# Attention with bias: score matmuls of two query chunks, whole transposes for pair 2 and the rests of q, shared output tiles, a new order

## The chip, the core and the metric

The kernel runs on one core of a Trainium2 chip. Its engines are named as on the profile's page: PE multiplies matrices (PEld are its weight loads, which run beside it), DVE and ACT compute elementwise, POOL computes elementwise too and here mostly issues transfers, and SP issues transfers. The metric is the device time of one execution in microseconds (us). Of a profiled execution there is also the span, from the first to the last instruction on the core.

## What is computed

Attention with an additive bias, for 4 batches of 8 heads, 1024 queries and keys, head dimension 64, in float32:

```python
scores = scale * np.matmul(q, k.transpose(0, 1, 3, 2))      # scale = 1 / 8
scores = scores + bias                                      # one bias for all heads
attn = np.exp(scores - scores_max) / (sum + 1e-8)
return np.matmul(attn, v)
```

## The kernel before

**Tiles.** Heads are taken in 16 pairs; each head's 1024 queries are 8 chunks of 128, and one unit of work, a *slot*, is one chunk of one head against all 1024 keys: 256 slots. PE multiplies keys by queries into PSUM as scores with the keys on the partitions, 8 blocks of 128 keys by 128 queries, which fill two PSUM banks (four blocks each). ACT takes the exponential of both banks into the ring `E` of 28 half slots (14 slots). PE then multiplies each block by the values: 8 matmuls of 65 columns, 64 of V and a column of ones that gives the row sums. Seven slots' outputs or fewer share one PSUM bank (`SIZES`); DVE takes the reciprocal of the sums, scales the bank and SP stores it.

**Bias.** A slot's bias is not added for each head. The operands of a head carry differences to the head before, so that scores build up in the banks: a first head of a group gets its bias by 8 matmuls with `ident8` (line 360), and every later head adds the product of two heads' stacked operands to what stands in the bank (line 363, `start=False`). So each pair needs four arrays of 128 rows by 1024: `ko`, `qo` (its own k and minus its q for the odd head) and `ke`, `qe` (stacked with the neighbour pair's), and for some pairs `qs` and `qz`. A place (0, 1 or 2) is a pair of banks, and three slots, a *round*, are under way at once. Slots 0 to 53 are the first pass (three chunks of the first 18 heads), slots from 54 on come after it.

**Preparing operands.** POOL loads k, q and v as bf16. Up to pair 6, k and q land with the two heads apart, and must be set side by side before a whole 128-column transpose: either DVE copies them into a `side` tile (`set_beside`, line 303), or PE transposes each head by itself (line 276, 64 columns, two instructions a block). From pair 7 on they land side by side. PE's transposes (line 270) go to PSUM, DVE copies them out as `ko` (line 284) or `qo` (line 286), and `ke`, `qe` are made by DVE copies (lines 295 and 297) or by SP's transfers (line 579). The chunks 3 to 7 of q of pairs 0 and 1 are loaded later, as rests.

**DVE's exponentials.** 29 of the 256 slots get their exponential from DVE in six steps: lines 401, 409, 413, 416, 419 and 422, the last of which writes the tile `de`.

**Order.** All engines work through their instructions in the order in which they are issued, and this order is a list of tokens written out in `ORDER`. `F` and `G` fill a slot's first and second bank; `X` is ACT's exponential of a slot, `P` and `Q` those of one and a half slots; `f r s h c l` are DVE's six steps; `A` is a slot's output matmuls; `T`, `C`, `D`, `S`, `N` are a transpose, its copy out, a doubling into `ke` or `qe`, a side copy and a negation, with `k` or `q` (or `r`, a rest) and the pair; `V` copies a landed v into place; `R` and `M` are a bank's reciprocal and scaling. Ahead of the list stands a head written out by hand (lines 482 to 532). POOL limits the loads under way: before a load it copies one element of an earlier one into `tick` (line 547).

## Time and profile before

| what | us |
|---|---|
| median of 3 runs (lowest, highest) | 226.67 (225.88, 227.08) |
| the profiled execution's own time | 226.95 |
| its span | 225.2 |
| ACT's first exponential begins, last one ends | 8.26, 220.06 |
| PE, DVE, ACT, POOL busy in the span | 215.4, 203.4, 212.5, 89.5 |

A row of the page gives the line, the engine, the operation, what it writes and reads with the shapes, the count, then busy time and the mean of one in ns, then idle time in front of it and what ended that. A row of a timeline gives start, length and the same names. A stretch's row gives its bounds, its length, each engine's busy time with the count of instructions that touch it, the granted clock of PE as a share, and figures of the transfers.

### The profile page before, as it was taken

Reading aid. Unit: us, or ns where it says so; the run is one execution under the profiler, and the core shown is the slowest. Engines: PE = TensorE matmul, PEld = TensorE weight load, DVE = VectorE, ACT = ScalarE, POOL = GpSimd, SP = SyncE. Lnnn points to the kernel's source line nnn. Section 1 sums busy time; section 2 is a strip of 40 time slices with the busy share of each in tenths; the row PEclk is TensorE's granted clock in tenths of the full one; section 3 lists DMA queues with packets and bytes.
Section 4 is the critical chain, followed back from the end, with each engine's and each line's share of the span. In section 5 each row is a group of like instructions: output and inputs, shape, how many; then the busy total and the mean of one; then the engine's idle time right before and its main releaser. Section 6 shows DMA issues by size and latency. Waiting matters only on the chain.

```text
span 225.2 us, 10307 instructions
## 1 busy us (share of the span) xinstructions
PE 215.4 (96%) x4535; PEld 206.5 (92%) x4535; DVE 203.4 (90%) x349; ACT 212.5 (94%) x225; POOL 89.5 (40%) x160
## 2 busy tenths in 40 slices
PE   7999999999999999999999997999999999999991
PEld 2879989999999999999999897999999999999891
DVE  3488798796999999999999999999999999999992
ACT  3799999999999999999999997999999999999990
POOL 8817568757557556306476653650000000000000
PEclk9999999999999999999999999999999999999998
DMA  6999999999999999899999999997112110212213
GB/s 197 217 205 215 230 216 156 188 172 174 140 123 150 108 132 97 114 151 175 167 183 202 116 185 177 97 154 77 45 45 58 27 42 20 73 39 66 56 50 100
DMA packets 88141, 28.95 MB, mean 129 GB/s; under 512 B 69216, under 2 KB 84832, under 8 KB 88096
## 3 DMA queue, kind: packets, MB, share of 16 engines
q0 software_dynamic: 62880, 14.06, 69.2%
q1 hardware_dynamic: 24512, 13.38, 23.4%
q10 hardware_dynamic: 704, 0.85, 1.2%
q8 instruction: 35, 0.57, 1.1%
q14 instruction: 10, 0.08, 0.1%
HBM read 29.36 MB, written 8.39 MB: 168 GB/s over the span
## 4 chain that ended last, share of the span: by engine, by line
ACT 32%; PE 9%; DVE 5%; DMA 5%; POOL 1%; issue 1%; DVEq 0%; POOLq 0%
ACT E L382 32%; PE pl L363 5%; PE po L443 4%; DMA k<-in_k_dram 3%; DMA q<-in_q_dram 2%; DVE dy L401 1%; DVE ds L413 1%; POOL tick L547 1%; DVE ob L475 1%; DVE qo L286 1%; POOL q L202 1%; DVE de L416 1%; DVE de L409 0%; DVE ko L284 0%; DVE q L309 0%
## 5 line engine op out<-in xcount | busy, mean ns | idle before, releaser
L382 ACT ACTIVATE E<-pl 128x1024 bf16<-128x1024 f32 (+2 forms) x221 | 209.4, 1075 | 3.4 <-PE pl L363 2.1
L443 PE MATMUL po<-vall,E 128*128 128x65 bf16 x1816 | 85.8, 194 | 0.1
L363 PE MATMUL pl<-qo,ko 128*128 128x128 bf16 x1024 | 77.5, 219 | 0.7 <-ACT E L382 0.6
L443 PEld LDWEIGHTS <-E 128*128 128x128 bf16 x1816 | 73.3, 98 | 0.3 <-DVE vall L628 0.2
L363 PEld LDWEIGHTS <-ko 128*128 128x128 bf16 x1160 | 68.5, 98 | 2.9 <-ACT E L382 1.1
L363 PE MATMUL pl<-qe,ke 128*128 128x128 bf16 x888 | 68.0, 219 | 1.4 <-issue 1.2
L363 PEld LDWEIGHTS <-ke 128*128 128x128 bf16 x888 | 51.9, 98 | 3.0 <-issue 1.6
L401 DVE TENSOR_SCALAR dy<-pl 128x1024 int32<-128x1024 f32 x29 | 35.3, 1218 | 2.8 <-PE pl L363 1.9
L422 DVE SCALAR_TENSOR_TENSOR de<-dy,ds 128x1024 uint16<-128x1024 int32 x29 | 34.9, 1213 | 0.0
L475 DVE TENSOR_TENSOR ob<-po,rs 128x448 f32<-128x448 f32 (+2 forms) x38 | 22.8, 601 | 0.5
L409 DVE TENSOR_SCALAR de<-dy 128x1024 f16<-128x1024 uint16 x29 | 19.6, 689 | 0.6 <-PE po L443 0.5
L202 POOL DMA_DIRECT2D q<-in_q_dram x18 | 15.9, 883 | 10.5 <-DVE qo L286 8.2
L413 DVE TENSOR_TENSOR ds<-de 128x1024 f16<-128x1024 f16 x29 | 19.6, 678 | 0.1
L419 DVE TENSOR_TENSOR ds<-ds,de 128x1024 f16<-128x1024 f16 x29 | 19.5, 679 | 0.1
L202 POOL DMA_DIRECT2D k<-in_k_dram x18 | 15.8, 880 | 8.1 <-PE px L270 4.7
L243 POOL DMA_DIRECT2D vall<-in_v_dram x18 | 16.8, 934 | 4.3 <-issue 3.6
L284 DVE COPY ko<-px 128x1024 bf16<-128x1024 bf16 (+1 forms) x16 | 10.7, 668 | 4.7 <-PE px L270 2.8
L286 DVE TENSOR_SCALAR qo<-px,sgn 128x1024 bf16<-128x1024 bf16 (+2 forms) x18 | 12.3, 684 | 2.5 <-PE px L270 1.5
L360 PE MATMUL pl<-ident,braw 128*128 128x128 bf16 x136 | 13.9, 227 | 0.0
L416 DVE TENSOR_SCALAR de<-de 128x1024 f16<-128x1024 f16 x29 | 13.0, 454 | 0.1
L443 PE MATMUL po<-vall,de 128*128 128x65 bf16 x232 | 12.1, 194 | 0.4 <-DVE ob L475 0.4
L360 PEld LDWEIGHTS <-braw 128*128 128x128 bf16 x136 | 11.1, 148 | 0.1
(63 smaller groups left out, 144.7 us busy)
## 6 DMA issues: line engine op xcount, KB each, us to landing
ke<-ko SPq DMA_DIRECT2D x20, 128.0 KB, 4.2
out_dram<-ob SPq DMA_DIRECT2D x40, 64.0 KB, 3.4
k<-in_k_dram POOLq DMA_DIRECT2D x18, 128.0 KB, 5.3
q<-in_q_dram POOLq DMA_DIRECT2D x18, 128.0 KB, 4.5
vall<-in_v_dram POOLq DMA_DIRECT2D x18, 128.0 KB, 5.4
out_dram<-ob SPq DMA_DIRECT2D x62, 32.0 KB, 2.6
braw<-in_bias_dram POOLq DMA_DIRECT2D x7, 256.0 KB, 5.4
v<-in_v_dram POOLq DMA_DIRECT2D x7, 256.0 KB, 6.3
```

The lines of the kernel that those rows point to most:

```text
L202: nc.gpsimd.dma_start(out=t[:, :, y, :], in_=(qf, kf)[x][pr][:, y].rearrange("p (c d) -> p c d", d=D))
L243: nc.gpsimd.dma_start(out=vall[:, (2 * pr + t) % VR, :, :D], in_=vf[pr][:, t])
L360: m = nc.tensor.matmul(to, braw[:, c, :].rearrange("p (kp kc) -> p kc kp", kc=NCH)[:, kc, :], ident8[:], start=i == 0, stop=False, skip_gr ...
L363: m = nc.tensor.matmul(to, kk[:, kc, :], qq[:, c, :], start=False, stop=True, skip_group_check=True)
L382: read(nc.scalar.activation(E[:, e0:e0 + n].rearrange("p b x -> p (b x)"), pl[:, b0:b0 + n].rearrange("p b x -> p (b x)"), ACTF.Exp, scale ...
L401: read(w.tensor_scalar(t["y"][:], pl[:, b:b + 2].rearrange("p b x -> p (b x)"), scale * LOG2E * 65536.0, CB * 65536.0, op0=ALU.mult, op1=A ...
L409: w.tensor_scalar(t["f"], t["lo"], CA / 65536.0, CA * CR, op0=ALU.mult, op1=ALU.add)
L413: w.tensor_tensor(t["s"], t["f"], t["f"], op=ALU.mult)
L419: w.tensor_tensor(t["s"], t["s"], t["f"], op=ALU.mult)
L422: w.scalar_tensor_tensor(t["e"].bitcast(U16).rearrange("p c q -> p (c q)"), t["y"][:], 1.0 / 512.0, t["s"], op0=ALU.mult, op1=ALU.add)
L443: nc.tensor.matmul(bank[b][:, banks[b].index(s), :], ehalf[s, kc // 4][:, kc % 4, :], vall[:, slots[s][2] % VR, kc, :], start=first and kc ...
L475: nc.vector.tensor_tensor(ob[:, :n, :], po[:, :n, :D], rs[:, :n, :].to_broadcast([P, n, D]), op=ALU.mult)
```

## The change

From slot 54 on, the slots of places 0 and 1 of a round are a *couple*: two neighbouring query chunks of one head. Place 0's banks now hold key blocks 0 to 3 of both chunks and place 1's banks blocks 4 to 7 of both. One score matmul has 256 moving columns, the two chunks, against one weight load. There are 68 such couples. An exponential covers half of the keys of both chunks, and an output's eight matmuls read both slots' exponentials.

```diff
+    couple = {}
     for s, x in enumerate(slots):
+        if s >= 6 * GROUPS[0] and x[0] < 2:
+            couple[s] = rounds[round_of[s]][:2]
...
+        n = 2 if s in couple else 1
+        if n == 2:
+            c = slots[couple[s][0]][1]
+        k0 = 4 * x + 2 * b if n == 2 else 4 * b
         for i in range(4):
-            kc = 4 * b + i
+            kc, c1 = k0 + i // n, c + i % n
...
+            elif i % n == 0:
+                m = nc.tensor.matmul(pl[:, 2 * x + b, i * P:(i + n) * P], kk[:, kc, :],
+                                     qq[:, c:c + n, :].rearrange("p c q -> p (c q)"), start=i == 0 and order[0] == "s",
+                                     stop=order[1] == "s", skip_group_check=True)
...
+    def weights(s, kc):
+
+        if s not in couple:
+            return ehalf[s, kc // 4][:, kc % 4, :]
+        return ehalf[couple[s][kc // 4], kc % 4 // 2][:, kc % 2 * 2 + couple[s].index(s), :]
```

Pair 2's k and q and the rests of q get side copies (`S`, now with a piece's chunks) and whole transposes; only pair 1 keeps the 64-column form. V's landings and DVE's output tiles share one pool of seven, in place of three and four. The tick copies go; a load's own issue waits for the earlier one. Loads of the second bias chunk and of pair 1's k change places.

```diff
-    def set_beside(pr, which):
+    def set_beside(pr, which, c0, n):
...
-    de = ctx.enter_context(tc.tile_pool(name="de", bufs=4))
+    de = ctx.enter_context(tc.tile_pool(name="de", bufs=7))
...
-            lands[pr, "v"] = vland.tile([P, 2, NCH, D], BF, name="v16")
+            lands[pr, "v"] = de.tile([P, NCH, P], BF, name="de").rearrange("p c q -> p (c q)").rearrange(
...
+                flight.append(do().ins)
                 if j >= 0:
-                    nc.gpsimd.tensor_copy(tick[:], flight[j])
-                flight.append(do())
+                    tc.add_manual_dep(flight[i], flight[j].name, DATA, reason="loads under way")
```

In the head, the cast of the second half of pair 0's k is split between ACT and DVE, the exponential's dependence on the ko copy is declared away, and the second round's exponential is taken bank by bank, its scores ahead of its bias. `ORDER` and `SIZES` are new throughout; the list's start as an example:

```diff
-F1 G1 F2 X1 G2 F3 X2 G3 Tk1a F4 X3 Ck1 G4 Tq1b F5 Dk1p0 X4 G5 Cq1 Tk2a Dq1p0 Dq1p1 X5 F6 Ck2 G6 F7 G7 X6 Tq2b F8 Cq2
+F3 G3 Tk1a X3 F4 Ck1 G4 F2 X4 Dk1p0 Tq1b G2 Cq1 Dq1p0 X2 Dk1p1 F6 G6 Sk2 X6 F5 G5 F7 Tk2a X5 G7 Sq2 F9 X7 Ck2 F8 G8
...
+        if not on:
+            tc.declare_no_dep(i, group="p", reason="another bank")
...
-        nc.scalar.copy(kr0[1].rearrange("p c t d -> p t c d"), k0f[:, :, half:])
+        nc.scalar.copy(kr0[1][:, :2].rearrange("p c t d -> p t c d"), k0f[:, :, half:half + 2])
...
+        nc.vector.tensor_copy(kr0[1][:, 2:].rearrange("p c t d -> p t c d"), k0f[:, :, half + 2:])
...
+        fill_half(1, 0, "s", "sb")
         fill_half(0, 1, "s")
         exp((0, 1))
+        fill_half(1, 0, "b", "sb")
+        exp((1, 0))
+        fill_half(1, 1, "s", "sb")
+        fill_half(1, 1, "b", "sb")
+        exp((1, 1))
```

In the rows below, what stands in brackets are the engines and queues for which an instruction waits. In the head, ACT's list before, from its first cast on (`dy` holds the landed inputs, `braw` the bias, `de` the cast k, `pl` the scores):

```order
L511 CAST braw<-dy 128x1024 [waits DMAHW1_49]
L512 CAST de<-dy 128x2x4x64 [waits DMAHW3_49]
L382 ACTIVATE E<-pl 128x512 [waits DVE_49,PE_49]
L382 ACTIVATE E<-pl 128x512 [waits PE_49]
L382 ACTIVATE E<-pl 128x1024 [waits PE_49] x20
```

and in the change:

```order
L513 CAST braw<-dy 128x1024 [waits DMAHW1_49]
L514 CAST de<-dy 128x2x2x64 [waits DMAHW3_49]
L382 ACTIVATE E<-pl 128x512 [waits PE_49] x4
L382 ACTIVATE E<-pl 128x1024 [waits PE_49] x14
L382 ACTIVATE E<-pl 128x1024
```

The cast of k is half as long, the first exponential no longer waits for DVE, and four short exponentials stand where there were two. The other half of that cast stands on DVE, ahead of the first `ko` copy:

```order
L512 CAST de<-dy 128x2x4x64 [waits DMAHW2_49]
L519 TENSOR_SCALAR qz_94<-px 64x384 [waits PE_49]
L520 CAST de<-dy 128x2x2x64 [waits DMAHW3_49]
L274 COPY ko<-px 128x512 [waits PE_49]
L274 COPY ko<-pl 128x512 [waits PE_49]
```

L520 is new there; the other four stood in this order before. On PE, at the start of the second pass, the end of a group of score matmuls (`ko` are the weights, `qo` the moving queries, `pl` the scores), before:

```order
L363 MATMUL pl<-qo,ko 128x128
L363 LDWEIGHTS ko
L363 MATMUL pl<-qo,ko 128x128
L443 LDWEIGHTS E
L443 MATMUL po<-vall,E 128x65 [waits DVE_49]
```

and in the change:

```order
L359 MATMUL pl<-qo,ko 128x256
L359 LDWEIGHTS ko
L359 MATMUL pl<-qo,ko 128x256
L359 LDWEIGHTS ko [waits Activation_49]
L359 MATMUL pl<-qo,ko 128x128
```

A couple's bank takes two matmuls of 256 columns; a slot of place 2 behind it still takes 128. On DVE, near the end of the first pass, where the rests of q come in (`vall` holds V in place, `dy` and `de` belong to DVE's exponentials, `po` is an output bank), before:

```order
L628 COPY vall<-v_259 128x16x64 [waits DMASW4_49]
L401 TENSOR_SCALAR dy<-pl 128x1024 [waits PE_49]
L286 TENSOR_SCALAR qo<-px,sgn 128x640 [waits PE_49]
L468 RECIPROCAL rs<-po 128x7
L297 TENSOR_SCALAR qz_98<-qo 64x640 [waits DVE_49]
L297 TENSOR_SCALAR qe<-qo 64x640
```

and in the change:

```order
L635 COPY vall<-de 128x16x64 [waits DMASW4_49]
L470 RECIPROCAL rs<-po 128x7 [waits PE_49]
L401 TENSOR_SCALAR dy<-pl 128x1024 [waits PE_49,Activation_49]
L477 TENSOR_TENSOR ob<-po,rs 128x448 [waits DMAHW6_49,DVE_49]
L293 COPY side<-qrest_251 128x2x5x64 [waits DMASW5_49]
L409 TENSOR_SCALAR de<-dy 128x1024
L413 TENSOR_TENSOR ds<-de 128x1024 [waits DVE_49]
L276 TENSOR_SCALAR qo<-px,sgn 128x640 [waits PE_49]
L287 TENSOR_SCALAR qz_94<-qo 64x640 [waits DVE_49]
L287 TENSOR_SCALAR qe<-qo 64x640
```

The side copy of the rest is new, and two steps of a DVE exponential now stand between it and `qo`. In the whole list PE has 7932 rows in place of 9072, and the 70 tick copies of POOL are gone.

More of the change, by code (lines that the diff above doesn't have):

```diff
@@ L133 @@
     warm = consts.tile([P, 1], F32)
-    tick = consts.tile([1, 1], BF)
     sgn = consts.tile([P, 1], F32)
@@ L176 @@
     assert sorted(x[1:3] for x in slots) == sorted((c, h) for c in range(NCH) for h in range(2 * NP))
-    first_slot = {}
-    last_slot, last_of = {}, {}
+    rounds = {}
+    for s, r in enumerate(round_of):
+        rounds.setdefault(r, []).append(s)
+    couple = {}
     for s, x in enumerate(slots):
-        first_slot.setdefault(x[2] // 2, s)
-        last_slot[x[2] // 2] = s
-        last_of[x[2]] = s
-    before = {}
-    at_place = {}
-    for s, x in enumerate(slots):
-        before[s] = at_place.get(x[0])
-        at_place[x[0]] = s
+        if s >= 6 * GROUPS[0] and x[0] < 2:
+            couple[s] = rounds[round_of[s]][:2]
+    assert all(slots[a][1:] == (slots[b][1] - 1,) + slots[b][2:] for a, b in couple.values())
     raws, lands, arrs = {}, {}, {}
@@ L223, in piece @@
             to = t[:, :, :cs.stop - cs.start, :]
-            nc.gpsimd.dma_start(out=to.rearrange("p t c d -> p t (c d)"),
-                                in_=qf[pr][:, :, cs.start * D:cs.stop * D])
-            return to[:1, 1, cs.stop - cs.start - 1, D - 1:]
+            return nc.gpsimd.dma_start(out=to.rearrange("p t c d -> p t (c d)"),
+                                       in_=qf[pr][:, :, cs.start * D:cs.stop * D])
         return [piece]
```

157 lines of the change are left out of this document (73 added, 84 removed).

## The prediction

> **What bounds the kernel now.** I read the page's busy shares first, then the groups by shape.
>
> ```profile
> span 225.2 us, 10307 instructions
> PE 215.4 (96%) x4535; PEld 206.5 (92%) x4535; DVE 203.4 (90%) x349; ACT 212.5 (94%) x225; POOL 89.5 (40%) x160
> L382 ACT ACTIVATE E<-pl 128x1024 bf16<-128x1024 f32 x205 | 189.8, 1053 | 2.4 <-PE pl L363 2.1
> L382 ACT ACTIVATE E<-pl 128x1536 bf16<-128x1536 f32 x14 | 19.2, 1473 | 0.0
> ```
>
> Three engines stand at 90% or more, so no share alone decides. ACT does little but exponentials, and its idle time in front of them is 2.4 us. How fast could it run? The next view cuts its time at every twelfth exponential (the count also takes in the two at the edges, so x14 holds twelve); the last row, from a second cut, holds five of the wide ones.
>
> ```profile
> 8.26:9.35 1.09, 1.09 (x3) 1.00 1.17 195
> 9.35:20.60 11.25, 11.13 (x14) 1.00 1.25 209
> 20.60:31.53 10.93, 10.93 (x14) 1.00 1.22 223
> 31.53:43.13 11.60, 11.11 (x14) 1.00 1.73 179
> 43.13:54.91 11.78, 11.47 (x14) 1.00 1.39 181
> 122.16:133.61 11.45, 11.21 (x14) 1.00 1.42 158
> 133.61:145.89 12.28, 11.11 (x14) 1.00 1.32 140
> 156.94:167.87 10.93, 10.93 (x14) 1.00 0.19 47
> ...
> 203.77:210.44 6.67, 6.67 (x6) 1.00 0.27 75
> ```
>
> The best stretches give 10.93 / 12 = 0.911 us for an exponential of 1024 columns and 6.67 / 5 = 1.334 for 1536. At that pace the 205 and 14 would need 186.8 + 18.7 = 205.5 us, and the two short ones took 1.09. From 8.26 to the last exponential's end at 220.06 there are 211.8, so **about 5.2 us are lost on ACT**, 8.3 lie before it and 5.1 behind. Against 10.93 the rows lose 0.32, 0.67 and 0.85 in the first pass (with 0.24 more up to 66.08: 2.1 in all), then 0.52 and 1.35 around 122 to 146; the other 1.2 is spread thinly. The chain of waits shows the largest:
>
> ```profile
> 128.69 0.26 PE po L443 x8
> 128.95 0.45 PE px L270 x8
> ...
> 138.41 0.17 PE pl L363
> 138.58 1.20 issue
> 139.78 0.58 PE pl L363 x7
> 140.38 63.37 ACT E L382 x68
> ```
>
> PE stopped for 1.20 us inside a group of eight score matmuls and waited for nothing that the profile shows; from 140.38 ACT alone carries the chain for 63 us. So the change can win only the 5.2 us, plus what it does to the head and the tail.
>
> **The head.**
>
> ```profile
> 6.62 0.62 ACT L512 CAST de<-dy 128x512 bf16<-128x512 f32 x1 [0.47 <-DMA dy<-in_k_dram]
> 6.80 0.42 DVE L284 COPY ko<-px 128x512 bf16<-128x512 bf16 x1 [0.23 <-PE px L270]
> 7.30 0.40 PE L270 MATMUL pl<-ident,de 128*128 128x128 bf16 x4
> 7.53 0.39 PE L363 MATMUL pl<-qz,ko 128*128 128x128 bf16 x4
> 7.73 0.42 DVE L284 COPY ko<-pl 128x512 bf16<-128x512 bf16 x1 [0.51 <-PE pl L270]
> 8.26 12.44 ACT L382 ACTIVATE E<-pl 128x512 bf16<-128x512 f32 x14 [1.01 <-DVE ko L284]
> ```
>
> The first exponential waits for the second ko copy although its own matmuls end at 7.92. The changed ACT list names PE alone there, which is worth 8.26 - 7.92 = 0.34. The cast at 6.62 is halved between ACT and DVE: ACT ends some 0.3 earlier, DVE puts about 0.28 (0.42 for 512 columns, halved, plus something fixed) ahead of its copy at 6.80, and 0.23 of that was idle. The transposes so start near 7.0, not 7.30; but the matmuls then wait for that copy, near 7.3, which leaves about 0.2 of the 0.3. The first two rounds become four short exponentials, 1.09 / 2 = 0.55 each against 0.91 for a whole one: 0.2 lost. I take **-0.45 us for the head** (bounds -0.6 and 0) and +0.2 for ACT's own work, in which 207 exponentials, 12 wide ones and four short ones need 188.6 + 16.0 + 2.2 = 206.8 against 186.8 + 18.7 + 1.1 = 206.6.
>
> **PE's work.**
>
> ```profile
> 1.20 4.37 PE L500 MATMUL pl<-E 128*128 128x512 bf16 x10 [1.20 <-DVE warm L488]
> 12.59 0.64 PE L276 MATMUL px<-ident,k 128*64 128x128 bf16 x16
> 17.84 0.61 PE L270 MATMUL px<-ident,side 128*128 128x128 bf16 x8
> ```
>
> From slot 54 on, 68 couples of slots with eight keys' blocks each turn 1088 score matmuls of 128 columns into 544 of 256. No row shows 256. The chain has 0.45 / 8 = 56 ns for 128 columns and 0.26 / 8 = 32 for 65. Two of 128 bound the new one at 112; a line through the two points gives 104; the 512-column form took 437 in the first 5 us, half of it 218. That last is far off: it would add 58 us, and columns went at 0.85 ns there against 0.44 later, so the place sets it rather than the width. I take 110, nearest to the 128-column row: 544 x 2 ns = 1.1 us (0 to 4.4). PE also drops 1140 rows of its list, 9072 to 7932. The whole transposes take 0.61 for what took 0.64: 52 half ones become 26, some 0.1. PE so saves **about 1.2 us out of 209**, thin over 150 us.
>
> Here a page says otherwise. The Trainium skill, "TensorE: Matmul & The Clock Gate", section "Back-to-back issue gap", gives 81 ns a matmul at 128 columns and 131 at 512 where each has its own weight load; an estimate from it for 256 is 98, so a couple would save 64 ns and PE 35 us. The trace disagrees: its loaded 128-column matmuls go at 56. By that page nothing would remain of ACT's waits on PE, which is the second case below.
>
> **DVE's work and the first pass.**
>
> ```profile
> 20.60:66.08 45.48, 44.39 (x933) 42.76 (x930) 39.06 (x76) 44.62 (x50) 28.70 (x57) 1.00 1.36 177
> 66.08:220.06 153.98, 152.09 (x3339) 149.80 (x3335) 151.62 (x241) 152.54 (x160) 47.40 (x79) 1.00 0.84 104
> ```
>
> ```profile
> L401 DVE TENSOR_SCALAR dy<-pl 128x1024 int32<-128x1024 f32 x29 | 35.3, 1218 | 2.8 <-PE pl L363 1.9 <-issue 0.2
> L422 DVE SCALAR_TENSOR_TENSOR de<-dy,ds 128x1024 uint16<-128x1024 int32 x29 | 34.9, 1213 | 0.0
> L409 DVE TENSOR_SCALAR de<-dy 128x1024 f16<-128x1024 uint16 x29 | 19.6, 689 | 0.6 <-PE po L443 0.5
> L413 DVE TENSOR_TENSOR ds<-de 128x1024 f16<-128x1024 f16 x29 | 19.6, 678 | 0.1
> L419 DVE TENSOR_TENSOR ds<-ds,de 128x1024 f16<-128x1024 f16 x29 | 19.5, 679 | 0.1
> L475 DVE TENSOR_TENSOR ob<-po,rs 128x448 f32<-128x448 f32 x30 | 18.6, 619 | 0.4
> L416 DVE TENSOR_SCALAR de<-de 128x1024 f16<-128x1024 f16 x29 | 13.0, 454 | 0.1
> L303 DVE COPY side<-q 128x1024 bf16<-128x1024 bf16 x4 | 2.2, 538 | 0.0
> ```
>
> DVE's third column in the first row says 39.06 busy of 45.48 us. Between the same exponentials (the 13th to the 60th) the new list has two side copies more and a V copy less (together 0.54), one closing pair (0.62 and a short one), and of DVE's own exponential one step each of L401, L409 and L413, two each of L416, L419 and L422: 0.54 + 0.62 + 1.22 + 0.69 + 0.68 + 0.91 + 1.36 + 2.43 = 8.4. Two L419 in a row take 1.28 where twice 0.68 would be 1.36, so about 0.08 of each overlaps; less 0.9, **+7.5**.
>
> ```profile
> 61.27 1.28 DVE L419 TENSOR_TENSOR ds<-ds,de 128x1024 f16<-128x1024 f16 x2
> ```
>
> That makes 46.6 in a stretch of 45.5: DVE is full. I cost this at nothing, because the outputs of slots 30 and 47 come 27 and 12 exponentials after their last steps in the new list, so chain steps may run late; what may not are the doublings (D), which stand one exponential, 0.9 us, ahead of the score matmuls that read them. If the cover is gone it costs up to 1.1 plus the waits that DVE cannot avoid, of 6.4 idle now. In return DVE has those 7.5 us less behind 66.08, where it is 151.62 of 153.98 busy. There ACT loses 3.1: the 1.2 us stop of PE, for which I take -0.9 (0 to -1.2: it is the only one of its length, and nothing shows why it should return or not), and 1.9 of thin losses, of which I take half, -1.0 (0 to -1.9), for a PE lighter by 1.2 and a DVE lighter by 7.5.
>
> The 70 tick copies on POOL go, and loads wait at their own issue; POOL is 40% busy, so nothing (if the loads come early, -0.3). V's landings in seven shared tiles take nothing: a load no longer waits for a V copy three loads back. Four stores and one ke copy more sit on SP's queue, hidden behind stores that nobody reads. The tail is the same: one output, reciprocal, scaling, store.
>
> **Sum against the profiled run:** 226.95 - 0.45 + 0.2 + 0 - 0.9 - 1.0 = 224.8. The profiled run lies 0.28 above the median of 226.67, so **224.5 on the median**, -1.0%. A measurement of this kernel can tell about 0.5%, 1.1 us, from no change.
>
> **Rivals.**
> - **ACT alone is the bound.** All 5.2 us go: 226.67 - 0.45 + 0.2 - 5.2 = 221.2. For it: DVE and PE get room behind 66 us. Against: the first pass gets none.
> - **The gain is hidden.** PE's 1.2 us are no one's last wait; the stop returns, and what the later part wins the full DVE takes in the first pass: head and ACT alone give -0.25, 226.4 (225.6 to 227.8).
> - **DVE becomes the bound from 20 to 66 us.** 46.6 of work plus half of its 6.4 idle is 49.8, so this stretch grows by 4.3: 226.67 - 2.15 + 4.3 = 228.8. It decides when D copies come over 0.9 us late; slower than before begins where DVE's waits there exceed 45.5 + 2.15 - 46.6 = 1.0 us beyond what late chain steps absorb. Against: at 151.62 of 153.98 it has run full behind 66 us with 3.1 lost in 154.
>
> **Chances:** forecast (223 to 226) 0.45; ACT alone 0.17; hidden 0.22; DVE bound 0.16. Below 225.5 fall most of the first and all of the second, 0.55; within 0.5% 0.28; above 227.8 0.17. The range 221.3 to 228.6 leaves about one in ten on each side, and takes in the bounds of the terms.
>
> **What would show it.** Right: the first exponential near 7.8; 256-column matmuls 108 to 112 ns apart; from 66 to 220 twelve exponentials in 10.95 or less; no stop of over 1 us on PE. Wrong: score matmuls in the first pass whose releaser is a DVE doubling or side copy; twelve exponentials in over 11.6 between 30 and 66; ACT waiting for outputs because both exponentials of a couple must be done; a couple's matmuls above 112 ns.

## The result, and the profile after

The changed kernel takes **227.63 us** (median of 9 runs, 226.78 to 228.91) against 226.67 of the kernel before in 9 runs beside it: ratio 1.0051, 95% interval 1.0028 to 1.0074, slower by half a per cent. The profiled execution took 227.62 with a span of 225.5, against 226.95 and 225.2. The direction was predicted wrong. The time lies in the stated range and in that of the rival "the gain is hidden" (225.6 to 227.8), about as far from its 226.4 as from the 228.8 of the rival "DVE becomes the bound".

The page's busy shares after, with the group of ACT's whole exponentials:

```profile
span 225.5 us, 9039 instructions
PE 215.3 (95%) x3965; PEld 197.5 (88%) x3965; DVE 206.3 (91%) x354; ACT 213.0 (94%) x227; POOL 72.5 (32%) x90
L382 ACT ACTIVATE E<-pl 128x1024 bf16<-128x1024 f32 x207 | 192.6, 1067 | 2.7 <-PE pl L359 2.2 <-PE po L445 0.3
```

The program has 1268 instructions fewer. ACT's idle time in front of whole exponentials, 2.4 us before, is 2.7. The two stretches whose DVE time the prediction worked out (bounds, length, then busy time of PE, PEld, DVE, ACT and POOL):

```profile
20.60:66.08 45.48, 44.46 (x905) 42.95 (x903) 44.69 (x88) 44.35 (x48) 25.05 (x30) 1.00 1.38 182
66.08:220.06 153.98, 152.09 (x2789) 140.05 (x2787) 147.74 (x231) 152.68 (x161) 34.64 (x39) 1.00 0.83 103
```

DVE went from 39.06 to 44.69 in the first and from 151.62 to 147.74 in the second: the shift of work happened. Between the same exponentials as in the prediction (the 13th to the 60th, here at 21.07 and 67.10) DVE is busy 45.24 of 46.03 us, so it has 6.2 more to do and not 7.5. PE's 152.09 behind 66 us did not move, though its list is shorter. ACT alone, cut at every 24 halves of `E` (twelve whole exponentials; the count also takes in those at the edges):

```profile
21.97:33.05 11.08, 11.08 (x13) 1.00 1.26 227
33.05:45.43 12.38, 11.56 (x13) 1.00 1.69 171
45.43:56.83 11.40, 11.13 (x13) 1.00 1.28 166
...
134.31:145.73 11.42, 11.08 (x14) 1.00 1.26 154
145.73:157.27 11.54, 11.24 (x14) 1.00 1.25 125
157.27:168.20 10.93, 10.93 (x13) 1.00 0.17 43
168.20:179.74 11.54, 11.22 (x14) 1.00 0.15 39
179.74:191.22 11.48, 11.16 (x14) 1.00 0.17 41
```

The 1.2 us stop of PE is gone: the row around 138 is 11.42 where it was 12.28. But the row from 33 us grew to 12.38, and four rows behind 134 lose 0.57 to 0.69 us each, where before the loss lay in the two rows from 122 to 146.

From here on a **loss** of ACT is the time between two starts of exponentials less the steady spacing of the sizes between them (0.904 us for 1024 columns, 1.331 for 1536, 0.478 for 512), counted from the 4th half on. The 124th half ends near 68 us, the 244th near 123, the 388th near 191:

| ACT's loss, us | to the 124th half | to the 244th | to the 388th | to the end | sum |
|---|---|---|---|---|---|
| before | 2.46 | 0.98 | 2.70 | 0.37 | 6.51 |
| after | 3.27 | 1.02 | 2.91 | 0.21 | 7.41 |

So the profiled difference of 0.67 is made up as follows: the last exponential ends 1.22 later (0.90 of loss, 0.11 of a later first exponential, the rest ACT's own work and the first four halves), the tail behind it is 0.88 shorter (5.13 to 4.25), and 0.33 more passes outside the span.

These are losses of single executions, but they go with the list. Up to the 124th half the new list loses 2.96 to 3.52 in seven profiles with its first pass as it is or nearly so (this one, e1, e2, e6, e9, e10 and e14 below; only e3, with the old head, has 2.48), the old one 1.58 to 2.46 in five (before, e4, e5, e11, e12).

Where the first pass's loss comes from is read from the chain of waits (start, length, what carried the chain). Of the changed kernel, from 36 us:

```profile
36.03 0.52 PE px L260 x8
36.55 1.21 DVE dy L401
37.76 0.66 DVE qo L276
38.42 0.51 DVE ke L285
38.93 0.33 DVE qe L287
39.26 0.34 DVE vall L635
39.60 0.97 DVE de L409
...
45.27 0.60 DVE ds L419
45.90 0.43 DVE qe L287
46.36 1.24 DVE de L422
47.64 0.43 PE po L445 x8
```

For eleven microseconds the chain runs from one DVE instruction to the next: doublings, q's and v's copies and exponential steps, end to end. PE waits at four points in this part of the first pass: for a copy of V at 32 us, for the reading of slot 30's banks at 37, for a copy of q at 43 and for a chain's last step at 47. ACT loses 0.25, 0.55, 0.37 and 0.40 there. The chain of the kernel before has no piece here, but that of e4 has, with the old list. It stays on PE throughout (the line numbers are e4's own):

```profile
36.69 0.45 PE px L264 x8
37.14 0.89 PE pl L357 x16
...
38.29 0.45 PE pl L357 x8
38.73 0.52 PE po L437 x16
39.25 0.45 PE px L264 x8
39.70 1.00 PE pl L357 x16
```

Behind 130 us the four losses are single waits. Two of them on PE's timeline (start, length, and in brackets the idle time before it and who ended it):

```profile
135.74 0.61 PE L260 MATMUL px<-ident,q 128*128 128x128 bf16 x8 [0.52 <-DVE ob L477]
148.96 0.43 PE L445 MATMUL po<-vall,de 128*128 128x65 bf16 x8 [0.55 <-DVE de L422]
```

At 136 the transposes of a q wait for the scaling that frees their bank; at 148 an output stands right behind the last step of its own chain. The other two, at 174 and 185, have no wait on PE that the timeline shows.

### The profile page after: what moved, and what is told of

It is laid out like the page before. It is cut to its first block, busy times and chain, and to the rows that moved or that the text cites. A ratio compares the mean times of both kernels' runs of the same rounds, so it can differ in the third digit from the quotient of the medians.

```text
span 225.5 us, 9039 instructions
## 1 busy us (share of the span) xinstructions
PE 215.3 (95%) x3965; PEld 197.5 (88%) x3965; DVE 206.3 (91%) x354; ACT 213.0 (94%) x227; POOL 72.5 (32%) x90
## 4 chain that ended last, share of the span: by engine, by line
PE 57%; DVE 17%; ACT 10%; DMA 3%; issue 2%; SPq 2%; DVEq 0%
PE pl L359 32%; PE po L445 20%; ACT E L382 10%; PE px L260 3%; DVE dy L401 3%; PE pl L356 3%; DVE de L409 2%; DVE de L422 2%; DMA qs<-q 2%; DVE qo L276 2%; DVE ob L477 2%; DMA qe<-q 1%; SPq L644 1%; DVE ds L413 1%; DVE ds L419 1%
## 5 line engine op out<-in xcount | busy, mean ns | idle before, releaser
L445 PE MATMUL po<-vall,E 128*128 128x65 bf16 x1816 | 87.1, 194 | 0.7 <-ACT E L382 0.3
L445 PEld LDWEIGHTS <-E 128*128 128x128 bf16 x1816 | 77.1, 98 | 3.4 <-issue 0.5
L359 PE MATMUL pl<-qo,ko 128*128 128x128 bf16 (+1 forms) x752 | 78.6, 239 | 1.2 <-DVE dy L401 0.6
L359 PE MATMUL pl<-qe,ke 128*128 128x128 bf16 (+1 forms) x648 | 68.1, 239 | 0.4 <-DVE qe L287 0.2
L359 PEld LDWEIGHTS <-ko 128*128 128x128 bf16 x856 | 57.9, 98 | 7.1 <-ACT E L382 2.5
L359 PEld LDWEIGHTS <-ke 128*128 128x128 bf16 x648 | 43.7, 98 | 4.7 <-ACT E L382 1.3
L477 DVE TENSOR_TENSOR ob<-po,rs 128x448 f32<-128x448 f32 (+3 forms) x38 | 22.9, 602 | 0.4
L197 POOL DMA_DIRECT2D q<-in_q_dram x18 | 17.4, 968 | 14.4 <-DVE rs L470 6.9
L409 DVE TENSOR_SCALAR de<-dy 128x1024 f16<-128x1024 uint16 x29 | 21.1, 740 | 0.1
```

Source lines behind the costliest of these rows:

```text
L197: return nc.gpsimd.dma_start(out=t[:, :, y, :], in_=(qf, kf)[x][pr][:, y].rearrange("p (c d) -> p c d", d=D))
L359: m = nc.tensor.matmul(pl[:, 2 * x + b, i * P:(i + n) * P], kk[:, kc, :], qq[:, c:c + n, :].rearrange("p c q -> p (c q)"), start=i == 0 an ...
L409: w.tensor_scalar(t["f"], t["lo"], CA / 65536.0, CA * CR, op0=ALU.mult, op1=ALU.add)
L445: nc.tensor.matmul(bank[b][:, banks[b].index(s), :], weights(s, kc), vall[:, slots[s][2] % VR, kc, :], start=first and kc == 0, stop=kc == ...
L477: nc.vector.tensor_tensor(ob[:, :n, :], po[:, :n, :D], rs[:, :n, :].to_broadcast([P, n, D]), op=ALU.mult)
```

## The experiments

All 18 in one table (ratio to the kernel before, measured beside each; loss columns as above, of one profiled execution each). The kernel before had medians of 226.6 to 227.4 beside them, so ratios compare the runs better than medians do. Of the edits the lines that matter are shown; `...` stands for what is left out. e9 to e13 leave a part of the computation out, and e5 mixes up its scores, as told below.

| run | median us | ratio, 95% interval | loss to 124th | to 244th | to 388th | sum |
|---|---|---|---|---|---|---|
| e1_uncoupled | 227.81 | 1.0058 (1.0033, 1.0083) | 2.96 | 1.80 | 3.02 | 8.00 |
| e2_half_transposes | 227.53 | 1.0038 (1.0012, 1.0063) | 3.38 | 1.43 | 2.86 | 7.88 |
| e3_old_head | 227.47 | 1.0046 (1.0024, 1.0068) | 2.48 | 1.02 | 2.78 | 6.49 |
| e4_no_ticks | 227.20 | 1.0019 (0.9995, 1.0043) | 2.12 | 2.42 | 1.82 | 6.72 |
| e5_order_before | 229.50 | 1.0125 (1.0081, 1.0169) | 2.18 | 2.12 | 2.95 | 7.77 |
| e6_second_mended | 228.67 | 1.0089 (1.0060, 1.0119) | 3.52 | 1.03 | 3.63 | 8.40 |
| e7_first_mended | 227.61 | 1.0036 (1.0006, 1.0066) | 2.51 | 1.01 | 3.51 | 7.24 |
| e8_both_mended | 228.50 | 1.0074 (1.0042, 1.0105) | 2.94 | 1.46 | 3.63 | 8.24 |
| e9_no_shift | 226.45 | 0.9985 (0.9963, 1.0007) | 3.06 | 0.90 | 2.43 | 6.60 |
| e10_seven_blocks | 227.20 | 1.0044 (1.0014, 1.0074) | 3.22 | 0.89 | 2.39 | 6.71 |
| e11_before_no_shift | 224.87 | 0.9934 (0.9910, 0.9959) | 2.37 | 0.99 | 1.11 | 4.84 |
| e12_before_seven_blocks | 226.21 | 0.9981 (0.9952, 1.0009) | 1.58 | 1.98 | 1.64 | 5.43 |
| e13_light_chains | 226.85 | 0.9995 (0.9972, 1.0018) | 2.21 | 1.04 | 2.88 | 6.34 |
| e14_second_again | 228.78 | 1.0071 (1.0043, 1.0098) | 3.02 | 1.17 | 3.46 | 7.84 |
| e15_all_again | 228.05 | 1.0041 (1.0021, 1.0062) | 2.69 | 1.01 | 3.45 | 7.34 |
| e16_good_places | 227.17 | 1.0006 (0.9983, 1.0028) | 3.10 | 1.01 | 2.46 | 6.78 |
| e17_slot_later | 231.09 | 1.0179 (1.0137, 1.0221) | 1.61 | 5.09 | 3.13 | 10.04 |
| e18_later_and_places | 230.55 | 1.0160 (1.0122, 1.0198) | 1.73 | 5.34 | 2.46 | 9.74 |

### Single parts undone

```diff
# e1: no couples
-        if s >= 6 * GROUPS[0] and x[0] < 2:
+        if False:
# e2: pair 2 and q's rests transposed by halves again
-... Sk2 ... Sq2 ... Sr0 ... Sr1 ...
# e3: the hand-written head of the kernel before; the list begins
+F1 G1 X1 F3 G3 Tk1a X3 F4 Ck1 G4 F2 X4
# e4: the kernel before without ticks
-                    nc.gpsimd.tensor_copy(tick[:], flight[j])
-                flight.append(do())
+                flight.append(do().ins)
+                    tc.add_manual_dep(flight[i], flight[j].name, DATA, reason="loads under way")
```

> The changed kernel with couples switched off: every slot holds its own chunk again, score matmuls have 128 columns throughout, the new order and all else stay. Theory 'order' (the couples give PE some 1.5 us, 512 to 544 pairs at 109 against 112 ns, and the loss sits in the new order): slower than the changed kernel by 0.7 to 2 us, 228.3 to 229.6. Rival 'couples' (outputs that wait for two exponentials cost more than PE saves): faster than the changed kernel, 226.0 to 227.2. If PE's time is nobody's last wait: 227.4 to 227.9.

> The changed kernel without the four new side copies: k and q of pair 2 and the two rests of q are transposed head by head in 64 columns as before, the order of all else stays. Theory 'DVE full in the first pass': DVE has 1.3 us less work there, the time falls by 0.4 to 1.3 us, 226.3 to 227.2, and the twelve exponentials from about 33 to 45 us take under 12.0 (12.38 in the changed kernel). Rival 'PE is the last wait in the first pass': the 64-column form costs PE some 0.6 us of switching, 227.6 to 228.3.

> The changed kernel with the hand-written head of before: ACT casts the whole second half of k, the first exponential depends on the ko copy again, the second round is one whole exponential with its bias first. Theory 'the new head gains 0.3 us, hidden in the profile by inputs that landed 0.5 us later': 227.8 to 228.2. Rival 'four short exponentials cost ACT more than the earlier start gives': 226.9 to 227.5.

> The kernel before with one edit: the 70 one-element copies that pace the loads go, and each load's own issue waits for the earlier load, as in the change. Theory: POOL is 40% busy and no load is late, 226.4 to 226.9 as before. Rival 'loads that come at other times collide with DVE and with the ke copies': slower by 0.5 us or more, 227.2 to 228.0.

No part by itself brings the time back: the medians of e1, e2 and e3 lie within 0.2 us of the changed kernel's, their ratios within 0.3 us. Without couples PE has 544 matmuls more to issue, and the time is the same (1.0058 against 1.0051). The losses at 136, 148, 174 and 185 stand in all three at the same places with nearly the same size (at 174 to 0.01 us), so they belong to the list. e2 was to show a first pass in which DVE is full: with the side copies gone the losses there should fall, and they don't (3.38). It took little off DVE, though: 44.67 us busy between 20 and 66 us where the changed kernel has 45.18. e3 loses 2.48 in the first pass, as little as the kernel before, with a chain that stands on DVE there as well; why isn't known. In e4, which keeps the old list, the profiled execution loses 0.86 and not 1.43 in the twelve exponentials around 139 us, and 1.43 in those from 89 to 101 us, where the kernel before loses 0.25: the stop that the prediction took for a single event at a place is a loss of the old list that wanders (in e12 it is 0.34 and 1.03 at the two places).

### The old list with the new parts

> The changed kernel with the list, the bank sizes and the hand-written head of the kernel before; 52 of its 68 couples stay (the other 16 would need an output of one slot before its partner's exponential, or after the E half is written again), and so do the shared output tiles and the loads without ticks. Theory A (the time sits in the order of the new list; the other parts are worth nothing): the time of the kernel before, 226.2 to 227.0, ACT's losses at about 54 and 138 us as before and none at 136, 148, 174 and 185. Theory B (the couples, the shared tiles or the direct waits of loads cost something that the first four runs did not single out): 227.3 or more with the old list. Theory C (the couples' 1.2 us of PE help where the list leaves DVE room): 225.9 or less.

This one didn't settle its question. The old list, bank sizes and head went into the changed kernel, with 52 couples. What a bank holds is carried on from head to head, so the 16 rounds left uncoupled add to banks laid out for couples, and scores mean nothing from there; the amount of work is the same. It took 229.5, and the trace shows two reasons of its own. The head waited 1.15 us for the bias chunk that the new load list puts behind k1. And at 175 us an output waited 0.52 for an exponential of ACT; 0.91 is lost in the twelve exponentials around it, where the kernel before loses 0.24. That it waited for the other half of its couple is likely, not shown. Another 1.12 is lost around 98 us, but e4 loses 1.43 there without a couple, so that is the old list's.

### Waits mended in the list, first try

```diff
# e6 (four places behind 130 us; two of them)
-Nq13 Tq15a X150 F154 Cq15 A146 G154 X149 F153
+Nq13 X150 F154 A146 G154 Tq15a X149 Cq15 F153
-r196 F199 G199 X195 F197 f199 G197
+F199 G199 X195 F197 f199 r196 G197
# e7 (four places in the first pass; two of them)
-M2 X29 G30 F31 G31 f30 Tq6b X31 F32 G32 A21a Cq6 X32 F33 G33
+X29 G30 F31 G31 f30 M2 Tq6b X31 F32 G32 Cq6 X32 F33 G33 A21a
-A25b R3 X38 F39 h24 F40 M3
+R3 X38 F39 h24 A25b F40 M3
# e8: both
```

> The changed kernel with four places of the list mended behind 66 us, where ACT lost .53 (136.1), .53 (148.4), .54 (173.7) and .46 (185.3), 2.06 together: the transposes of q15 behind the next score matmuls and not right behind the scaling that frees their bank; the output of slot 155 two outputs later than its chain's last step; DVE's second reading of score banks (slot 199) ahead of the f16 step of slot 196; one of five outputs in a row behind the score matmuls that ACT waits for. Theory A (each of these waits is a price of its own): 1.5 to 2.1 us come back, 225.5 to 226.2, and the four losses are each below 0.2. Rival D (PE and DVE are so full that a wait taken away comes back a few exponentials later): 227.2 or more, with new losses between 130 and 200 us.

> The changed kernel with four places of the list mended ahead of 66 us, where ACT lost .25 (33.1), .55 (37.0), .37 (43.2) and .39 (47.3), 1.56 together: an output of pair 3 behind the next score matmuls, DVE's reading of slot 30's banks ahead of the scaling of bank 2, the first output of bank 4 and the output of slot 24 each behind score matmuls. The amount of DVE's work stays. Theory A: 0.9 to 1.5 us come back, 226.1 to 226.8. Rival D (DVE has 44.7 of 45.5 us busy here, so the work itself is the bound and the waits move): 227.2 or more, and the stretch from the 13th to the 60th exponential stays at 45.4 or longer.

> All eight places mended at once. Theory A: the sum, 2.4 to 3.6 us back, 224.0 to 225.2, faster than both kernels. Rival D: 227 or more.

Theory A fell as it was put. In e6 the place at 136 went from 0.53 to 0.24 and stayed so, but at 174 the loss kept its 0.54 and a new one of 0.62 came behind it, where PE waits for the next reading of banks; that the step put off for the first reading made this one late is likely, not shown:

```profile
176.93 0.61 PE L359 MATMUL pl<-qo,ko 128*128 128x256 bf16 x4 [0.65 <-DVE dy L401]
```

In e7 the loss to the 124th half fell by 0.76, in e8, with the same four places, by 0.33 (e7's profile has a late head, as the last section tells). In e7 0.60 came back between the 244th and the 388th half, at 128 and 137 us, where PE waited for a scaling by DVE. A mended wait was worth a part of itself or less.

### One engine made lighter

```diff
# e9 (changed kernel) and e11 (kernel before): the shift step left out
-                chain[s].pop(0)()
+                step = chain[s].pop(0)
+                if kind != "h":
+                    step()
# e10 and e12: seven key blocks in an output
-        for kc in range(NCH):
+        for kc in range(NCH - 1):
...
-                             start=first and kc == 0, stop=kc == NCH - 1, skip_group_check=True)
+                             start=first and kc == 0, stop=kc == NCH - 2, skip_group_check=True)
```

> The changed kernel without the shift step (L416, 0.45 us each) of DVE's 29 exponentials, so DVE has 13 us less to do, 4 of the 29 in the stretch from 20 to 66 us; the values of DVE's slots are then not exponentials. Theory D (DVE, being full, sets the losses): ACT's losses shrink by 2 us or more, first where DVE is fullest (1.5 at 36 to 45 us) and at the four places behind 130 us, and the time is 225.5 or less. Rival P (PE is the bound behind 66 us, DVE is only where the last wait happens to end): less than 0.7 off, 227 or more. Rival O (the order: a wait falls where an instruction stands behind an unlucky one in its queue, whatever the load): the four places behind 130 us keep over half of their 2.1 us.

> The changed kernel with seven of the eight key blocks in each output (256 matmuls of 65 columns and their weight loads fewer, 33 ns each: 8.3 us off PE, evenly spread; the last block of keys is left out of the outputs). Theory D: less than 0.7 us off. Rival P: 2 us or more off, 225.6 or less, and losses behind 66 us shrink most. Rival O: the four places keep over half of their 2.1 us.

> The kernel before without the shift step of DVE's 29 exponentials (13 us off DVE, nearly all behind 66 us; the values of DVE's slots are then not exponentials). Theory D: as DVE was 151.6 of 154.0 us busy behind 66 us, its losses there (4.0, 1.4 of it the stop at 138) shrink by 1.5 or more: 225.2 or less. Rivals P and O: 226 or more.

> The kernel before with seven of the eight key blocks in each output (8.3 us off PE; the last block of keys is left out of the outputs). Rival P: 2 us or more off, 224.7 or less. Theory D and rival O: 226 or more; what remains of the stop at 138 shows whether PE's load has a part in it.

This is the clearest result. With **8.3 us less on PE** (256 matmuls of some 33 ns) both kernels gain 0.4 us by their medians; by the ratios it is 0.4 in the kernel before and 0.2 in the changed one, both within the noise. With **13 us less on DVE** (29 steps of 0.45; its busy time falls by 9.5 to 9.7) the kernel before gains 1.8 and the changed one 1.2 by the medians, 1.5 each by the ratios, of which 0.35 in the changed one lies outside the span. So PE's load is next to no one's bound, and DVE's is a bound, in part. (In its one profiled execution e12 loses 1.08 less on ACT than the kernel before; its median shows 0.4.) In the kernel before the lighter DVE takes the whole wandering loss away: 1.11 instead of 2.70 up to the 388th half, and ACT's idle time in front of whole exponentials falls from 2.4 to 0.9:

```profile
L382 ACT ACTIVATE E<-pl 128x1024 bf16<-128x1024 f32 x205 | 189.8, 1051 | 0.9 <-PE pl L363 0.5
```

In the changed kernel the losses at 136 and 148 go from 0.57 and 0.69 (by stretches of twelve exponentials) to 0.13 and 0.35 in e9 and to 0.23 and 0.62 in e10, while the one at 127 rises from 0.24 to 0.55 in e9. Those at 174 and 185 keep 0.69 or 0.70 and 0.62 or 0.63 with either engine made lighter: the load of neither makes them. The first pass is not helped by e9 either (3.06), as only four of the 29 shifts fall in it.

### DVE made lighter in the first pass alone

```diff
# e13
-            w.scalar_tensor_tensor(... 1.0 / 512.0, t["s"],
+            w.scalar_tensor_tensor(... 1.0 / 512.0, t.get("s", t["f"]),
...
-                chain[s].pop(0)()
+                step = chain[s].pop(0)
+                if s > 47 or kind not in "shc":
+                    step()
```

> The changed kernel without the square, shift and cube steps of DVE's first four exponentials (slots 24, 30, 44 and 47; their values are then not exponentials): 4 x 1.81 = 7.2 us off DVE, all of it between 30 and 68 us, which is what the new list put there on top of the old one's. Theory D1 (that stretch is full on DVE and this is where its loss of 3.3 us against 2.5 of the kernel before is from): ACT loses 2.4 us or less up to the 124th half (about 67 us), and 0.8 to 1.3 us come back, 226.3 to 226.8. Rival O (the waits at 33, 37, 43 and 47 us fall where instructions stand in the queues: the reading of slot 30's banks behind a scaling, an output behind a copy): they stay, 1.0 us or more of their 1.56, and the time stays within 0.5 of 227.6.

The loss to the 124th half falls from 3.27 to 2.21, below the 2.46 of the kernel before, and the stretches from the 268th half on stay to the hundredth (0.57, 0.69, 0.09, 0.69 and 0.63 again). The ratio falls from 1.0051 to 0.9995, some 1.3 us, with 0.35 us of it outside the span. A part of the 1.06 may come from a late head: the first exponential is at 9.43 here and at 8.37 in the changed kernel. e14 below, whose list is the changed one's up to 122 us, has it at 9.39 and loses 3.03, so 0.8 is the safer figure for DVE's part. DVE is busy 40.92 us between 20 and 66 us, where the same stretch of the changed kernel has 45.18:

```profile
20.00:66.00 46.00, 45.42 (x933) 44.52 (x933) 40.92 (x79) 45.54 (x50) 24.59 (x30) 1.00 1.40 186
```

And its chain of waits around the same place runs over PE, with a single DVE reading in it:

```profile
37.06 0.47 PE px L260 x8
37.53 1.22 DVE dy L401
38.80 0.84 PE pl L359 x12
39.64 0.26 PE po L445 x8
39.90 0.22 PE pl L359 x4
40.12 0.45 PE px L260 x8
40.57 0.45 PE pl L359 x8
41.02 0.26 PE po L445 x8
```

So with the load that the new list put there the chain leaves DVE and the loss falls to that of the old list. Between 36 and 48 us the chain stands on DVE, wholly or for more than half, in every profile with the new list and all four exponentials of the first pass; it stands on PE or ACT, with about a tenth on DVE at most, in the old list (e4, e5, e11, e12) and where the first pass has less for DVE (e13, e17, e18). What the new list loses there above the old one is therefore DVE's load. One of the four waits stays: for the reading of slot 30's banks 0.53 of 0.55 are still lost in e13. The relief doesn't reach beyond: a DVE made lighter early leaves the later places as they were.

### Second tries at the places, and one slot moved

```diff
# e14 (five places behind 122 us; three of them), e15 = e14 + e7
-A130 r136 G140 Tq14b R18 M18 X140
+A130 G140 Tq14b R18 M18 r136 X140
-G168 A160 A157a X168 F172 G172 s152 F167 A158 X172
+G168 A160 X168 F172 G172 A155 s152 F167 A157a X172 A158
-G212 A196 X212 s209 F215 G215 R28 h209 F214 X215 c209 G214 M28 F216 X214 R29 G216 l209 F218 X216 G218
+G212 F216 X212 G216 A196 s209 F215 X216 G215 R28 h209 F214 X215 c209 G214 M28 X214 R29 l209 F218 G218
# e16: three places of e7, those at 127 and 136 of e14, and at 148
+G168 A160 X168 F172 G172 A155 s152 X172 F171 R22 G171 c136 F167 A157a G167 A158 r164 A165 X171
# e17: slot 24 to ACT, slot 98 to DVE (two places of the list); e18 = e17 + e16
-X22 f24 F26
+X22 X24 F26
-F98 Tq9a X97 G98 A92 Cq9 F99 X98 A94 G99
+F98 X97 G98 F99 G99 f98 Tq9a A92 X99 Cq9 F100 G100 A94 r98
```

> The changed kernel with five places behind 66 us in another order. At 127: the closing of bank 18 ahead of the f16 step of slot 136. At 136: as in the second try before (it went from .53 to .24 there). At 148: both outputs behind the score matmuls of the round after the next. At 174: the score matmuls of slot 196 ahead of an output, and both f16 steps behind the third reading of banks by DVE in a row (196, 199, 198), since nothing but that chain of readings and refills stood there whether DVE or PE was made lighter. At 185: the third slot of the next round between the two that had to refill one bank pair within a single exponential. Rival O: each wait goes, losses behind 66 us fall from 3.8 to 2.3 or less, 225.8 to 226.5. Theory S (what is late is the whole of DVE's queue, so a wait comes back one or two closings later): 227.2 or more. If the place at 174 or 185 keeps its .5, its cause is not the one named.

> The five places of the run before it, and the four of the first pass that were mended earlier (there ACT's loss up to the 124th half fell from 3.3 to 2.5 and came back at 128 and 137 us, two places that are mended here). Rival O: 224.9 to 225.8, faster than both kernels. Theory S: 227 or more.

> The changed kernel with only those places mended that held in the tries before (three in the first pass, 127 and 136 us), and the one at 148 in a third form: each pair of score matmuls directly behind the exponential that frees its banks, and the outputs in the holes between. 174 and 185 are left as they are. If a wait is bound to its place and the new place is free: ACT's loss falls from 7.4 to 6.2 or less and 0.8 to 1.3 us come back, 226.3 to 226.9. If what is won is lost again behind it, as in the tries before: 227.2 or more.

> The changed kernel with ACT taking slot 24 and DVE slot 98 in its place, so that DVE has one exponential (5.3 us) less between 30 and 42 us and one more between 97 and 110, where the trace of the changed kernel has DVE idle for most of its 2.8 us between 66 and 130; DVE's and ACT's work in all is unchanged. Theory D1 (the first pass is too full on DVE): ACT's loss up to the 124th half falls by 0.8 or more (from 3.3; ACT has one exponential more there, so the 124th half itself comes at about the same time), and the time falls by 0.5 to 1.3 in all if the later place has room for it: 226.3 to 227.1. If the later place has none: losses of 0.5 or more between 95 and 130, and no gain.

> Both: slot 98 instead of 24 on DVE, and the places of the run two before this one. If the two gains add: 225.0 to 226.2, faster than the kernel before by up to 0.7%. If DVE is only shifted: 227 or more.

In e14 and e15 the places at 127 and 136 held (0.11 and 0.35 in e15, from 0.24 and 0.57), while those at 148, 174 and 185 rose from 0.69, 0.69 and 0.63 to 0.91, 0.84 and 1.15. The causes that I had put to 174 and 185, three readings by DVE in a row and one bank pair refilled within an exponential, are so not shown. e16 kept what had held: its loss is 6.78, and its time that of the kernel before (1.0006). The waits at 127 and 136 go when their places are mended, which gives about 0.35 us together; the one at 148 moved on by some 4 us.

e17 tells the most. Up to the 124th half it loses 1.61, half of what the changed kernel loses there. But behind it DVE had no room for another exponential. From its view of ACT alone, the two stretches from 89 us:

```profile
88.89:102.83 13.94, 11.75 (x13) 1.00 0.67 114
102.83:115.09 12.26, 11.23 (x13) 1.00 1.07 141
```

These lose 3.09 and 1.45 where the changed kernel loses 0.21 and 0.25. On PE's timeline the waits for DVE follow each other: for a copy of k, a scaling, a reading of banks, and an output at the end of a chain:

```profile
96.84 0.42 PE L445 MATMUL po<-vall,de 128*128 128x65 bf16 x8 [0.45 <-DVE ko L274]
99.44 0.61 PE L260 MATMUL px<-ident,k 128*128 128x128 bf16 x8 [0.31 <-DVE ob L477]
100.82 0.62 PE L359 MATMUL pl<-qo,ko 128*128 128x128 bf16 x8 [0.33 <-DVE dy L401]
103.89 0.30 PE L445 MATMUL po<-vall,de 128*128 128x65 bf16 x4 [1.06 <-DVE de L422]
```

The 2.8 us that DVE is idle between 66 and 130 us in the changed kernel are the gaps between waits and not room for the some 5 us of an exponential (its six steps' means add up to 4.98). No run beat the kernel before with the whole of the computation.

## Why the prediction was wrong

**The steps that failed** are two terms of the sum.

- *The first pass at nothing.* "I cost this at nothing, because the outputs of slots 30 and 47 come 27 and 12 exponentials after their last steps in the new list, so chain steps may run late." The working up to there was right in kind: 46.6 us of DVE's work were expected in a stretch of 45.5, and it came to 45.24 in a stretch that grew to 46.03. But the chain shows copies out, doublings and readings of banks in one row with the exponential's steps; each of them waits behind whatever stands ahead of it on DVE, and PE waits for some of them. The prediction watched the doublings, for which PE waits 0.2 us in all; the waits came for a copy of V, a reading, a copy of q and a late last step. It cost 0.81 of loss against the kernel before, and e13 gives back 0.8 to 1.06 when the steps go. This is the mechanism of the rival "DVE becomes the bound", with 0.8 us where that had put 4.3.
- *The stop and half of the thin losses, -1.9.* Behind the 124th half ACT lost 4.05 us before and 4.14 after: nothing came back. This is the larger miss. PE's half of the reason falls with e10 and e12, in which 8.3 us off PE are worth 0.4 at most. DVE's half does not: in the old list a lighter DVE is worth 1.5 to 1.8 us (e11). But the new list brought four waits of its own, 2.6 us by stretches. Two of them shrink when DVE is made lighter (e9); those at 174 and 185 don't, and their cause stays open.

The sum forecast -2.15 for the profiled execution and +0.67 was measured. Of the 2.82 between them 0.81 is the first pass, 1.99 the later losses, 0.56 the head and 0.33 time outside the span; a tail shorter by 0.88 goes the other way. That the time lies in the stated range is so in part luck: neither the tail nor the time outside the span was in the sum.

Of the signs named beforehand, the 256-column matmuls (109 ns) and the absent stop came as for a right forecast. The first exponential (8.37, not 7.8) and the rows behind 134 us (up to 11.54, not 10.95) did not, and one sign of a wrong one came in full: twelve exponentials in 12.38 from 33 us.

**Term by term:**
- *Head, -0.45.* The mechanism came true, the landing took it back. From the last cast of k to the first exponential it takes 1.17 us where it took 8.26 - 6.62 = 1.64, which is -0.47:

```profile
7.20 0.41 ACT L514 CAST de<-dy 128x256 bf16<-128x256 f32 x1 [0.72 <-DMA dy<-in_k_dram]
8.37 1.78 ACT L382 ACTIVATE E<-pl 128x512 bf16<-128x512 f32 x3 [0.76 <-PE pl L359]
```

  But that cast begins at 7.20 instead of 6.62, since k landed later. With the new load list (k1 ahead of b2) it began at 6.73 to 7.47 in sixteen profiled executions, with the old one at 6.49, 6.62, 6.63 and 7.02 (e11, before, e4, e12). That the load list does it may be and wasn't tried by itself. e3, with the old head and the new loads, took 0.16 us less than the changed kernel, so the new head's 0.47 is not seen in the time either; PE's pace in the head, which differs by about 1 us between executions (last section), may hide it.
- *ACT's own work, +0.2.* By the steady spacings 0.1.
- *PE's work.* The size was right, and the worth of it was not. In the chain six couple matmuls take 0.66 us:

```profile
63.96 0.66 PE pl L359 x6
```

  That is 0.11 each, as taken (their starts are 109 ns apart in the median, those of 128 columns 56). But the 1.2 us "off PE" were half of the argument for getting thin losses back, and e1, e10 and e12 say that PE's load is no bound: 8.3 us are worth 0.4 at most, so 1.2 are worth 0.06 at most. The rule of the Trainium skill, "TensorE: Matmul & The Clock Gate", section "Back-to-back issue gap", with 81 ns at 128 columns, would have made the couples worth more; the trace disagrees, with 56 and 109 ns. The isolated gap that the Trainium skill gives in the same section, N / 2.4 + 2.5, makes an estimate of 109 for 256; the trace agrees, with 109.
- *The stop, -0.9.* It went, and the stretches from the 244th to the 388th half still lose 2.91 instead of 2.70. The old list's stop was not an event of one place: in e4 the loss lies elsewhere, and in e11, with a lighter DVE, it is gone. The new list lost it and got four waits.
- *Thin losses, -1.0.* 0.98 became 1.02 between the 124th and the 244th half; nothing was recovered, although DVE is 3.9 us less busy behind 66 us. (The prediction's 5.2 us of loss on ACT are 6.5 by the steady spacing, since its best stretch, 10.93, holds losses too.)
- *First pass, 0.* +0.81, as above.
- *Ticks, shared tiles and whole transposes, 0.* e2 doesn't speak against it. e4, without ticks, is 0.4 us slower by its ratio, within the noise, and its time outside the span is 0.36 longer. The shared tiles weren't tried alone.
- *Tail, 0.* -0.88 in the profiled execution. Others of the old list have tails of 4.47 to 4.81 (e4, e11, e12), so part of it is that execution's own.
- *Outside the span.* Not in the sum at all: 0.35.

The rival "the gain is hidden", given 0.22, came closest in kind: PE's saving is no one's last wait, and the full DVE takes time in the first pass. But the stop did not return, and there was no gain behind it to be taken. What misled was the reading of ACT's 5.2 us as a reserve that any relief would draw on.

## What to carry to other kernels

Where three engines are over 90% busy, shares and idle times don't tell which load is a bound. Leaving out a few per cent of one engine's work (13 us of 206, 8.3 of 215 here) does, in one run an engine, and it tells it by stretch. Work moved onto an engine that becomes full is not free because its own result is late enough: count what stands behind it in that engine's queue. And a wait that the timeline named was worth a part of its length at most here; mend it and look for it again 10 us later before adding it to a sum.

## What was not expected of the hardware

**Time outside the span goes with the kernel.** The time of an execution less its span is 1.78 us (median) in the kernel before, over all runs, and 2.13 in the changed one (2.08 to 2.18 in nine runs). Each kernel has its own value with a spread of some 0.15: e2, e9, e11, e12 and e13 have 1.77 to 1.80; e3 and e5 2.01 and 1.98; e1, e4, e6 to e8, e10 and e14 to e18 2.10 to 2.17. That is a third of the difference measured between the two kernels, and no view of the profile shows it. It isn't the order of the list alone (e9 and e13 have the changed one's) and not the count of PE's instructions (e1). Small edits switch it either way: the ticks left out of the kernel before (e4) bring 0.36 more, and four side copies left out of the changed one (e2) 0.33 less. What sets it stays open.

**The head differs between executions, by landings and more by PE's pace.** The changed kernel's head, unaltered, had its first exponential at 7.88 in the profile of e1 and at 9.55 in that of e7, and 1.06 of these 1.67 us are left where the last exponential ends. The last cast of k begins 0.68 later in e7. The rest is PE: the same eight bias matmuls in e1 and in e7 are

```profile
6.73 0.66 PE L356 MATMUL pl<-ident,braw 128*128 128x128 bf16 x8
7.60 1.06 PE L356 MATMUL pl<-ident,braw 128*128 128x128 bf16 x8
```

In e7, and so in e3, e13 and e14, matmuls of 128 columns start 107 ns apart until 10 us or a little later; in the other profiles it is 55 to 65 ns from 7 us on. The page's granted clock is 1.00 from 7 to 10 us in e1 and e7 alike, so it doesn't show this. The same step is seen in the first matmuls of the program: those of 512 columns start 427 ns apart, the last ones of the changed kernel and of e1 217 and 216. What sets the time of the step stays open. A single profiled execution can't show half a microsecond in the head.
